# A 3x3 convolution with residual add: weights loaded on 128 partitions from another queue, the first image load split by columns over two queues, six early stores instead of five

## The chip, the cores and the metric

The kernel runs on one core of a Trainium2 chip. The metric is the device time of one execution in microseconds (us); medians are given with the lowest and highest of the runs. A profiled execution also gives the span, from its first to its last instruction. For the kernel before the time is about 2.1 us above the span.

## The reference

```python
def reference(x, weight, residual):      # x, residual [16, 64, 64, 64] f32; weight [64, 64, 3, 3] f32
    ... # pad x by one pixel on each side
    output[b, co] += weight[co, ci, kh, kw] * x_pad[b, ci, kh:kh+h, kw:kw+w]   # for all b, co, ci, kh, kw
    return (output + residual).astype(np.float32)
```

Each of x, residual and the output is 16.78 MB, the weights are 147 KB: 50.48 MB have to cross between HBM (the chip's main memory) and SBUF (the core's own memory, whose rows, 128 in the image tiles here, are called partitions).

## The kernel before

Images are worked on in pairs. A pair's image tile and residual tile are 128 partitions of 16 KB; the queue of SP, the sync engine, issues all loads and stores but that of the weights, which is on ScalarE's queue. ScalarE casts the image to bf16, TensorE multiplies, VectorE adds the product to the residual tile in place, and SP stores that tile. The parts that matter here:

```python
    ident = pool.tile([64, 64], FP32)
    ro = [pool.tile([128, NPIX], FP32, name=f"ro{p}") for p in range(NPAIR)]
    xr = [nc.alloc_sbuf_tensor(f"xr{i}", [128, NPIX], FP32) for i in range(NXR)]
    wraw = nc.alloc_sbuf_tensor("wraw", [64, 576], FP32)
    ...
        for p in range(NPAIR):                       # SP: all loads ...
            if p >= NXR:
                nc.sync.wait_ge(s_half, 2 * (p - NXR) + 3)
            i = load_x(p)
            if p == 0:
                to_the_front(i)                      # issued at entry, ahead of the start barrier
            load_ro(p)
        for p in range(NEARLY):                      # ... then five early stores
            nc.sync.wait_ge(s_add, 2 * p + 3)
            store(p).then_inc(s_out, 16)
    ...
        nc.scalar.dma_start(out=wraw[:, :], in_=w_flat[:, :]).then_inc(s_w, 16)
    ...                                              # VectorE: six weight casts out of PSUM
        for half, d, par, kh in blocks:
            i = nc.vector.tensor_copy(out=wl[hp, d, :, par, :], in_=tpf[0:64, 3 * kh : 3 * kh + 3, :])
    ...
    for p in range(NEARLY, NPAIR):                   # issued only when all compute is done
        store(p)
```

## Time and profile before

| | before |
|---|---|
| time, median (lowest to highest) | 124.1 us (124.02 to 124.42) |
| span | 122.1 us |
| bytes moved, steady rate | 50.48 MB, 429 GB/s |
| busy: PE, VectorE, ScalarE | 86.5, 75.2, 62.0 us |
| first packet starts, last data packet ends | 1.01 us, 120.75 us |

The page of the profile has one row of 40 slices for the DMA engines and one for their GB/s. The reading here is by stretches: wherever the rate is below 429 GB/s the stream loses time that it never gets back, because the transfers set the end. The trace also has a record for each packet, with its start, duration and size. A packet here is one row of a tile, mostly 16 KB. The lines are shown in the prediction.

### The profile page before, as it was taken

Reading aid. Unit: us, or ns where it says so; the run is one execution under the profiler, and the core shown is the slowest. Engines: PE = TensorE matmul, PEld = TensorE weight load, DVE = VectorE, ACT = ScalarE, POOL = GpSimd, SP = SyncE. Lnnn points to the kernel's source line nnn. Section 1 sums busy time; section 2 is a strip of 40 time slices with the busy share of each in tenths; the row PEclk is TensorE's granted clock in tenths of the full one; section 3 lists DMA queues with packets and bytes.
Section 4 is the critical chain, followed back from the end, with each engine's and each line's share of the span. In section 5 each row is a group of like instructions: output and inputs, shape, how many; then the busy total and the mean of one; then the engine's idle time right before and its main releaser. Section 6 shows DMA issues by size and latency. Waiting matters only on the chain.

```text
span 122.1 us, 729 instructions
## 1 busy us (share of the span) xinstructions
PE 86.5 (71%) x389; PEld 10.4 (9%) x105; DVE 75.2 (62%) x38; ACT 62.0 (51%) x33; POOL 2.2 (2%) x16
## 2 busy tenths in 40 slices
PE   0003799999999999999999999999999930000000
PEld 0003000101111010101010101111110100000000
DVE  0004101989889898898989889898798988000000
ACT  4009948966984993992994896699000000000000
POOL 5100000000000000000000000000000000000000
PEclk9999999999999999999999999999999999555555
DMA  6999999999999999999999999999999999999993
GB/s 182 408 348 429 429 429 429 429 424 429 429 429 424 429 429 429 429 429 429 429 429 419 429 429 424 429 429 429 435 435 435 429 429 429 435 435 429 429 429 140
DMA packets 3536, 50.48 MB, mean 413 GB/s; under 512 B 400, under 2 KB 400, under 8 KB 464
## 3 DMA queue, kind: packets, MB, share of 16 engines
q1 hardware_dynamic: 3456, 50.33, 97.8%
q10 hardware_dynamic: 80, 0.15, 0.4%
HBM read 33.70 MB, written 16.78 MB: 413 GB/s over the span
## 4 chain that ended last, share of the span: by engine, by line
PE 70%; DVEq 2%; DVE 2%; issue 0%
PE ps L84 53%; PE ps L83 17%; DVEq L118 2%; DVE ro L182 2%
## 5 line engine op out<-in xcount | busy, mean ns | idle before, releaser
L182 DVE TENSOR_TENSOR ro<-ps,ro 64x2048 f32<-64x2048 f32 x32 | 73.2, 2289 | 17.4 <-PE ps L84 16.9
L84 PE MATMUL ps<-xp,wl 128*128 128x504 bf16 (+1 forms) x288 | 79.9, 387 | 0.2
L159 ACT CAST xp<-xr 64x2048 bf16<-64x2048 f32 x16 | 30.3, 1896 | 21.3 <-DMA xr<-in_x_dram 21.1
L83 PE MATMUL ps<-xp,wl 128*128 128x504 bf16 (+1 forms) x92 | 35.6, 387 | 2.4 <-PEq L200 2.4
L163 ACT CAST xp<-xr 64x2048 bf16<-64x2048 f32 x16 | 30.4, 1897 | 0.4
L83 PEld LDWEIGHTS ps<-xp,wl 128*128 128x128 bf16 x96 | 9.5, 99 | 77.5 <-issue 77.5
L172 DVE CAST wl<-ps 64x192 bf16<-64x192 f32 x6 | 1.9, 347 | 10.9 <-PE ps L195 10.8
L195 PE MATMUL ps<-ident,wraw 64*64 64x64 f32 x9 | 1.1, 305 | 9.6 <-DMA wraw<-in_weight_dram 9.6
L159 ACT ACT_TABLE_LOAD x1 | 1.3, 1283 | 1.5 <-SPq L118 1.5
L195 PEld LDWEIGHTS ps<-ident,wraw 64*64 64x64 f32 x9 | 0.9, 163 | 9.6 <-issue 9.6
L146 POOL MEMSET xp<- 64x64 bf16 x4 | 0.6, 147 | 0.2
L145 POOL MEMSET xp<- 64x64 bf16 x4 | 0.6, 145 | 0.2
L148 POOL MEMSET wl<- 64x192 bf16 x1 | 0.3, 253 | 0.1
L147 POOL MEMSET wl<- 64x192 bf16 x1 | 0.3, 252 | 0.1
L135 POOL TENSOR_SCALAR_AFFINE_SELECT ident<-ident 64x64 f32<-64x64 f32 x1 | 0.2, 233 | 0.2 <-POOL ident L133 0.2
L133 POOL MEMSET ident<- 64x64 f32 x1 | 0.1, 145 | 0.5 <-SPq L118 0.5
L235 POOL MEMSET const-bfloat16-1.0<- 128x1 bf16 x1 | 0.1, 113 | 0.0
L235 POOL MEMSET const-uint8-127<- 128x1 uint8 x1 | 0.1, 112 | 0.0
L235 POOL MEMSET const-float32-1.0<- 128x1 f32 x1 | 0.1, 109 | 0.0
L235 POOL MEMSET const-float32-0.0<- 128x1 f32 x1 | 0.1, 104 | 0.2 <-issue 0.2
## 6 DMA issues: line engine op xcount, KB each, us to landing
xr<-in_x_dram SPq DMA_DIRECT2D x8, 2048.0 KB, 17.6
ro<-in_residual_dram SPq DMA_DIRECT2D x8, 2048.0 KB, 22.1
out_dram<-ro SPq DMA_DIRECT2D x8, 2048.0 KB, 28.7
wraw<-in_weight_dram ACTq DMA_DIRECT2D x1, 144.0 KB, 8.5
```

What stands on the lines that cost most here:

```text
L83: return e.matmul(out=out_, lhsT=lhsT, rhs=rhs, start=start, stop=stop, skip_group_check=True)
L84: return e.add_instruction(mybir.InstMatmult(name=nc.get_next_instruction_name(), engine=PE, ins=[e.lower_ap(rhs), e.lower_ap(lhsT)], outs ...
L118: with tc.tile_critical(no_gpsimd_drain=True):
L145: nc.gpsimd.memset(t[0:64, 0, :], 0.0).then_inc(s_id, 1)
L146: nc.gpsimd.memset(t[64:128, J, :], 0.0).then_inc(s_id, 1)
L147: nc.gpsimd.memset(wl[0:64, 0, :, 1, :], 0.0).then_inc(s_id, 1)
L159: i = nc.scalar.copy(out=t[64:128, 0:J, :], in_=x4[hp, :, 0, :])
L163: nc.scalar.copy(out=t[0:64, 1 : J + 1, :], in_=x4[hp, :, 1, :]).then_inc(s_pack, 1)
L172: i = nc.vector.tensor_copy(out=wl[hp, d, :, par, :], in_=tpf[0:64, 3 * kh : 3 * kh + 3, :])
L182: i = nc.vector.tensor_tensor(out=o4[hp, :, par, :], in0=psj[64 * par : 64 * par + 64, :, :], in1=o4[hp, :, par, :], op=ADD)
L195: i = nc.tensor.transpose(out=ps[0][0:64, t // 8, t % 8, :], in_=wraw3[:, :, t], identity=ident[:, :])
L235: nc = _bacc.Bacc("TRN2", target_bir_lowering=False, num_devices=1)
```

## The change

Its intent: load the weights through all 128 partitions and early on SP's queue, share the first image load between both queues, prepare the weights on VectorE and ScalarE together, and keep one more store in the queue at the end.

```diff
-    NEARLY = 5
+    NEARLY = 6
-    w_flat = weight.rearrange("co ci kh kw -> co (ci kh kw)")
+    w_rows = weight.rearrange("co (h ci) kh kw -> (co h) (ci kh kw)", h=2)
-    ident = pool.tile([64, 64], FP32)
+    ident = pool.tile([128, 128], FP32)
-    wraw = nc.alloc_sbuf_tensor("wraw", [64, 576], FP32)
+    wraw = nc.alloc_sbuf_tensor("wraw", [128, 288], FP32)
...
-            i = load_x(p)
             if p == 0:
-                to_the_front(i)
+                to_the_front(load_x(p, cols=slice(0, NPIX // 2)))
+                nc.sync.dma_start(out=wraw[:, :], in_=w_rows[:, :]).then_inc(s_w, 16)
+            else:
+                load_x(p)
...
+        nc.gpsimd.wait_ge(s_id, 2)
...
-        nc.scalar.dma_start(out=wraw[:, :], in_=w_flat[:, :]).then_inc(s_w, 16)
+        to_the_front(load_x(0, nc.scalar, slice(NPIX // 2, NPIX)))
...
+            if n == 0:                               # ScalarE: four of the twelve weight casts
+                nc.scalar.wait_ge(s_wt, 1)
+                for b in blocks[4:]:
+                    for h in range(2):
+                        i = nc.scalar.copy(**weight_block(h, *b))
+                i.then_inc(s_wt, 1)
...
+        for k, b in enumerate(blocks[:4]):           # VectorE: eight of them
+            for h in range(2):
+                i = nc.vector.tensor_copy(**weight_block(h, *b))
...                                                  # nine transposes of 128x32 instead of 64x64
+        nc.tensor.wait_ge(s_wt, 3)
```

More of the change, by code (lines that the diff above doesn't have):

```diff
@@ L68, with load_x @@
     s_add = sem("s_add")
-    def load_x(p):
-        return nc.sync.dma_start(out=xr[p % NXR][:, :], in_=x_bc[128 * p : 128 * p + 128, :]).then_inc(s_x[p % NXR], 16)
+    def load_x(p, engine=nc.sync, cols=slice(0, NPIX)):
+        return engine.dma_start(out=xr[p % NXR][:, cols], in_=x_bc[128 * p : 128 * p + 128, cols]).then_inc(
+            s_x[p % NXR], 16
+        )
     def load_ro(p):
@@ L113, in to_the_front, with weight_block @@
         at = next(
-            i for i, e in enumerate(front) if e.engine == mybir.EngineType.SP and isinstance(e, mybir.InstDrain)
+            i for i, e in enumerate(front) if e.engine == ins.engine and isinstance(e, mybir.InstDrain)
         )
         front.insert(at, copy.replace(ins, ins=[fixed(a) for a in ins.ins], outs=[fixed(a) for a in ins.outs]))
+    blocks = ((0, 0, 0, 0), (1, 0, 0, 1), (1, 0, 1, 0), (0, 1, 1, 1), (0, 1, 0, 2), (1, 1, 1, 2))
+    tp = ps[0].rearrange("p c j w -> p c (j w)")
+    def weight_block(h, half, d, par, kh):
+        at = 64 * half + 32 * h
+        return dict(out=wl[at : at + 32, d, :, par, :], in_=tp[0:32, kh, 0:384].rearrange("p (kw co h) -> p kw co h", kw=3, h=2)[:, :, :, h])
     with tc.tile_critical(no_gpsimd_drain=True):
@@ L140 @@
             base=0,
-            pattern=[[-1, 64]],
+            pattern=[[-1, 128]],
             channel_multiplier=1,
         ).then_inc(s_id, 1)
+        nc.gpsimd.wait_ge(s_id, 2)
         for t in xp:
@@ L157 @@
             if im == 0:
-                nc.scalar.wait_ge(s_x[p % NXR], 16 * (p // NXR + 1))
+                nc.scalar.wait_ge(s_x[p % NXR], 16 * (p // NXR + 1 + (p % NXR == 0)))
             i = nc.scalar.copy(out=t[64:128, 0:J, :], in_=x4[hp, :, 0, :])
@@ L163 @@
             nc.scalar.copy(out=t[0:64, 1 : J + 1, :], in_=x4[hp, :, 1, :]).then_inc(s_pack, 1)
-        nc.vector.wait_ge(s_wt, 1)
-        tpf = ps[0].rearrange("p c j w -> p (c j) w")
-        blocks = ((0, 0, 0, 0), (1, 0, 0, 1), (1, 0, 1, 0), (0, 1, 0, 2), (0, 1, 1, 1), (1, 1, 1, 2))
-        for half, d, par, kh in blocks:
-            hp = slice(64 * half, 64 * half + 64)
-            i = nc.vector.tensor_copy(out=wl[hp, d, :, par, :], in_=tpf[0:64, 3 * kh : 3 * kh + 3, :])
-        i.then_inc(s_bank, 2)
+            if n == 0:
[4 more added lines that the diff above has]
+                i.then_inc(s_wt, 1)
+        nc.vector.wait_ge(s_wt, 1)
+        for k, b in enumerate(blocks[:4]):
+            for h in range(2):
+                i = nc.vector.tensor_copy(**weight_block(h, *b))
+                if k == h == 0:
+                    i.then_inc(s_bank, 2)
+        i.then_inc(s_wt, 1)
         for n in range(B):
@@ L194 @@
         for t in range(9):
-            i = nc.tensor.transpose(out=ps[0][0:64, t // 8, t % 8, :], in_=wraw3[:, :, t], identity=ident[:, :])
+            i = nc.tensor.transpose(
+                out=tp[0:32, t // 3, 128 * (t % 3) : 128 * (t % 3) + 128], in_=wraw3[:, :, t], identity=ident[:, :]
+            )
         i.then_inc(s_wt, 1)
+        nc.tensor.wait_ge(s_wt, 3)
         with nc.Fori(0, B // NXP, 1, engines=[PE]):
```

## The prediction

The sum: -0.43 us for the weights, +0.10 for the packets and -0.10 for the split, together -0.43, from 124.1 to 123.7 us. The weights' term stands as the estimate, 80% of the 0.54 us that the trace loses between 5.8 and 8.9 us. The low end of the range, 123.1, was for all of that gain and a faster start.

> **What bounds the kernel now.** I read the summary page first: its row of slices, its queues and its groups.
>
> ```profile
> span 122.1 us, 729 instructions
> ...
> DMA  6999999999999999999999999999999999999993
> GB/s 182 408 348 429 429 429 429 429 424 429 429 429 424 429 429 429 429 429 429 429 429 419 429 429 424 429 429 429 435 435 435 429 429 429 435 435 429 429 429 140
> ...
> q1 hardware_dynamic: 3456, 50.33, 97.8%
> q10 hardware_dynamic: 80, 0.15, 0.4%
> ...
> L182 DVE TENSOR_TENSOR ro<-ps,ro 64x2048 f32<-64x2048 f32 x32 | 73.2, 2289 | 17.4 <-PE ps L84 16.9
> ```
>
> The transfers are the bound. All 40 slices but the first and last have the DMA engines at 90% or more, and from the fourth slice on they move 429 GB/s without a break. The program moves 50.48 MB whatever the compute does; at 429 GB/s that is 117.7 us of the 122.1 us span. PE, VectorE and ScalarE are busy for 86.5, 75.2 and 62.0 us, all of it beside the transfers. So only three things can move the end: when the first byte starts, how many bytes' worth of time the stream loses on its way, and what follows the last byte.
>
> The second view is the table of stretches of time (columns: stretch, its length, busy us of PE, PE loads, VectorE, ScalarE, GpSimd with instruction counts, granted clock, DMA share, GB/s).
>
> ```profile
> 1.00:3.00 2.00, 0.00 (x0) 0.00 (x0) 0.00 (x0) 1.28 (x1) 1.39 (x10) 1.00 1.03 270
> 3.00:5.80 2.80, 0.00 (x0) 0.00 (x0) 0.00 (x0) 0.00 (x0) 0.60 (x3) 1.00 0.97 409
> 5.80:8.90 3.10, 0.00 (x0) 0.00 (x0) 0.00 (x0) 0.01 (x1) 0.00 (x0) 1.00 1.03 354
> 8.90:12.00 3.10, 1.14 (x9) 0.93 (x9) 1.16 (x4) 3.08 (x2) 0.00 (x0) 1.00 0.99 423
> 12.00:119.80 107.80, 85.40 (x380) 9.52 (x96) 74.01 (x35) 57.61 (x31) 0.00 (x0) 0.92 1.01 429
> ```
>
> The stream loses time in two places, both before 9 us. **Start:** the first packet begins at 1.06 us; from then to 3.00 at 429 GB/s would be 832 KB, 540 KB were moved, so 0.68 us are lost, and from 3.0 to 5.8 another 2.8 x 20/429 = 0.13. The transfer records (one for each packet, with start, duration and size) say why: the first packet on each engine takes 0.78 to 1.78 us, where a 16 KB packet later takes 0.611. **Weights:** from 5.8 to 8.9 the rate is 354, a loss of 3.1 x 75/429 = 0.54 us, although the share of busy engines is full. The weight packets (64 of 2304 B, on ScalarE's queue) begin at 5.25 and end at 8.31; in that time the 16 KB packets of the other queue stretch from 0.61 to 0.75-0.92 us, and they are back at 0.61 by 8.9. The loss goes with the weights, not with the image.
>
> The third view is the timeline, at the entry, the weight path, and the last issue of stores.
>
> ```profile
> 0.00 0.38 SPq L71 DMA_DIRECT2D xr<-in_x_dram  x1
> ...
> 0.95 0.53 ACTq L151 DMA_DIRECT2D wraw<-in_weight_dram  x1
> ...
> 8.89 1.90 ACT L159 CAST xp<-xr 64x2048 bf16<-64x2048 f32 x1 [6.09 <-DMA xr<-in_x_dram]
> 9.60 0.93 PEld L195 LDWEIGHTS ps<-ident,wraw 64*64 64x64 f32 x9 [9.60 <-issue]
> 9.63 1.14 PE L195 MATMUL ps<-ident,wraw 64*64 64x64 f32 x9 [9.63 <-DMA wraw<-in_weight_dram]
> 10.81 1.97 DVE L172 CAST wl<-ps 64x192 bf16<-64x192 f32 x6 [10.81 <-PE ps L195]
> ...
> 98.78 4.61 DVE L182 TENSOR_TENSOR ro<-ps,ro 64x2048 f32<-64x2048 f32 x2 [0.58 <-PE ps L84]
> 103.68 1.76 SPq L77 DMA_DIRECT2D out_dram<-ro  x3
> ```
>
> The compute chain (weights, transposes, casts, then matmuls without a gap from 13.1 to 98.8, last add done at 103.4) releases only the last three stores, issued at 103.68. The last packet of data ends at about 120.8; three stores are 6.29 MB or 14.7 us, so the queue still holds earlier stores until about 106.1. With 1.06 us from issue to first packet, as at the entry, the compute chain has some 1.4 us of slack before the queue runs dry. From the last data to the end of the span is 1.3 us; the timed 124.1 is 2.0 above the span.
>
> [...] In this trace the issue takes 0.38 us and is followed by 0.7 us before the first packet, so the split of the first load has little to save.
>
> **The change part by part.**
> *Weights on 128 partitions.* The same 147 KB as 128 packets of 1152 B. [...]most of its 0.54 us goes; I count 80% of it, -0.43. More packets cost their fixed part: a 2304 B packet undisturbed takes 93 ns, against 86 ns at the rate of 16384 B in 611; so some 8 ns a packet. Four more weight packets on each engine, eight more from the halved image rows and one more semaphore write are 13 x 8 ns = +0.10. The weights are issued second by SP, at about 1 us, and the residual load about 0.5 us later than now; the queue holds 2 MB of image (4.9 us) by then, so this is hidden.
> *Image 0 by columns on both queues, at entry.* 128 packets of 8 KB on each queue instead of 128 of 16 KB. Bytes and engines are the same. Each engine could have the slow first packets of two queues open together. If the first-packet delay is a latency, it overlaps and nothing is won or lost; if it grows with size, up to 0.3 is won. I count -0.10.
> *Weight preparation.* Nine transposes stream 128 columns instead of 64: the present pitch is (1.14 - 0.3)/8 = 0.11 us, doubled 0.21, so about 1.14 + 9 x 0.105 = 2.1 us, +0.95. The casts become 12 of 32x192; [...]0.347 us each by the group of L172 (1.97 us for six in a row, 0.33 apart). VectorE does eight: 2.6 us, +0.7. ScalarE does four after its two image casts: about 4 x 0.35 = 1.4 us (an estimate from VectorE's). PE now waits for both. With the image landing about 1.2 us earlier (7.7: no weights among it) and weights about 8: transposes to 10.1, VectorE to 12.7; ScalarE 7.7 + 3.8 = 11.5, then to 12.9. So matmuls begin near 13.0 instead of 13.1, or up to 1 us later if the loads don't come earlier. Either way it is off the path that sets the end, as long as the final stores are issued in time.
> *Six early stores.* Store 5 needs thirteen semaphore counts, which VectorE gives at 103.4 - 3 x 5.19 - 2.3 = 85.5 us. It is then in the queue long before its turn, and only two stores wait for the end of the program's compute block: two are 9.8 us, so the slack grows from 1.4 to about 6.3 us. It gains nothing now; it keeps the queue full if the stream moves forward by 0.5 us or the compute chain back by 1 us.
> *Sum:* -0.43 + 0.10 - 0.10 = -0.43 us, from 124.1 to **123.7 us**. The whole that could be had here is the 0.68 + 0.13 + 0.54 = 1.35 us lost at the head, which is 1.1%.
>
> **The rivals.**
> *Small packets or two queues[...] cost the time.* The slow stretch may come from an engine alternating between two queues, or from small packets as such. For: the stretch is the only time in the trace when two queues run together. Against: the first dozen weight packets, 5.25 to 5.6 us, leave the 16 KB packets at 0.611. Then the change makes it worse: 16 packets an engine alternate in the image instead of four, or twice as many small packets run; losing the 0.54 again once over gives 124.6.
> *The start is what improves.* Two queues bring twice the first packets; if the 0.7 us is per packet and not per engine, the stream fills about 0.3 to 0.5 us sooner[...]. Against: the first 16 packets already occupy all 16 engines at 1.06 to 1.5 us.
> *The compute chain becomes the bound.* If matmuls began 1 us later with five early stores, the queue would run dry for a few tenths; with six there are over 5 us to spare, so this rival gives +0.
> *Nothing shows.* The runs before spread from 124.02 to 124.42, as wide as my gain.
>
> **Range and chances.** [...]the loss of the first rival in part 124.4; I put 8 in 10 on 123.1 to 124.4. Two per cent is 2.5 us: below 121.6 would need more than all head losses together, above 126.6 a stall that I see no cause for. Chances: faster 0.02, same 0.96, slower 0.02.
>
> **What would show it.** In the changed profile the third slice should be near 420 GB/s instead of 348, and the stretch from 5.8 to 8.9 us above 410, with 16 KB packets at 0.61 us; the first ScalarE cast should start near 7.7 instead of 8.89; transposes should take about 2.1 us; the first conv matmul should begin at 12.9 to 14; the late slices should stay at 429 with two stores issued near 104; and the last data should end about 0.4 us earlier. I am wrong if the rate still sags while the weights are moved, if the first slices are slower with two queues, if first packets appear much later or earlier than 1.06 us, or if the rate drops after 104 us.

## The result

The kernel after takes **122.98 us** (122.92 to 123.00, six runs), against 124.10 before (124.02 to 124.42, six runs). The ratio is 0.9905, 95% interval 0.9892 to 0.9918. Ratios are computed as the mean time of one kernel's runs over that of the other's of the same rounds, so they are not quite the ratio of the medians quoted. The prediction said 123.7 in a range of 123.1 to 124.4: the direction was right, the gain was more than twice the forecast, and the time fell just outside the range.

The page of the kernel after, in the rows that answer to those of before:

```profile
span 121.2 us, 736 instructions
...
DMA  6999999999999999999999999999999999999993
GB/s 168 427 444 433 433 433 433 433 427 433 433 427 427 433 433 427 427 433 427 433 433 433 433 433 422 433 389 433 433 433 433 422 433 433 433 433 433 427 433 151
...
q1 hardware_dynamic: 3600, 49.43, 96.3%
q10 hardware_dynamic: 144, 1.05, 2.0%
...
L189 DVE CAST wl<-ps 32x192 bf16<-32x192 f32 x8 | 2.8, 348 | 10.4 <-PE ps L214 10.3
...
L182 ACT CAST wl<-ps 32x192 bf16<-32x192 f32 x4 | 1.2, 306 | 0.0
```

The third slice rose from 348 to 444 GB/s. The first slice fell from 182 to 168, and the first row below from 270 to 254, though the prediction named slower first slices as a sign of being wrong. It isn't one: these views count a packet's bytes where it starts, so the long packets of before count earlier. By the packets' ends 0.5 MB had passed at 3.29 us, against 3.58 before. There is a new dent (the word for this loss below), 389 GB/s in the 27th slice (about 79 to 82 us), that before doesn't have. (The 433 against 429 in the other slices is no rate: slices are shorter with a shorter span, and the same packets fall into each.) The queue of ScalarE, q10, now carries half an image pair.

The table of stretches of the kernel after (columns as in the prediction: the last one is GB/s):

```profile
1.00:3.00 2.00, 0.00 (x0) 0.00 (x0) 0.00 (x0) 1.28 (x1) 1.32 (x8) 1.00 0.95 254
3.00:5.80 2.80, 0.00 (x0) 0.00 (x0) 0.00 (x0) 0.00 (x0) 0.85 (x5) 1.00 1.00 421
5.80:8.90 3.10, 0.76 (x4) 0.58 (x5) 0.00 (x0) 1.13 (x1) 0.00 (x0) 1.00 1.06 439
8.90:12.00 3.10, 1.32 (x7) 0.58 (x4) 1.60 (x5) 3.06 (x4) 0.00 (x0) 1.00 1.01 433
```

The stretch from 5.8 to 8.9 us, where the weights pass, went from 354 to 439 GB/s: the sag is gone.

The timeline of the kernel after (columns: start, us, engine, line, operation, what ended the idle time before):

```profile
0.00 0.38 SPq L71 DMA_DIRECT2D xr<-in_x_dram  x1
0.13 0.36 ACTq L71 DMA_DIRECT2D xr<-in_x_dram  x1
...
7.77 1.90 ACT L173 CAST xp<-xr 64x2048 bf16<-64x2048 f32 x1 [5.41 <-DMA xr<-in_x_dram]
...
8.14 2.08 PE L214 MATMUL ps<-ident,wraw 128*32 128x128 f32 x9 [8.14 <-DMA wraw<-in_weight_dram]
...
10.33 2.90 DVE L189 CAST wl<-ps 32x192 bf16<-32x192 f32 x8 [10.33 <-PE ps L214]
11.50 1.26 ACT L182 CAST wl<-ps 32x192 bf16<-32x192 f32 x4
...
13.66 0.59 PE L85 MATMUL ps<-xp,wl 128*128 128x512 bf16 x1 [3.44 <-PEq L222]
...
104.42 0.96 SPq L79 DMA_DIRECT2D out_dram<-ro  x2
```

The image lands 1.1 us earlier and the weights 1.5 us earlier, but their preparation takes longer, so the matmuls begin 0.5 us *later* than before and the last stores are issued 0.7 us later. None of this empties the queue: by the packet records some packet is always moving between the first and the last.

**Where the time came from.** From the packet records one can say when the first N MB had been moved:

| moved | before | after | difference |
|---|---|---|---|
| 1.5 MB | 5.96 us | 5.67 us | -0.29 |
| 4 MB (weights past) | 12.38 | 11.56 | -0.82 |
| 32 MB (end of loads) | 77.74 | 76.57 | -1.17 |
| 33.8 MB (first stores) | 81.92 | 81.08 | -0.84 |
| last data packet | 120.75 | 119.87 | -0.89 |

So 0.29 us is won at the start, 0.53 at the weights and 0.35 little by little over the long load phase (in before the packets are slightly longer there, which is called the creep below), and 0.33 is given back where loads turn into stores. The span is 0.9 us shorter (122.1 to 121.2). The time is 1.12 us shorter; the rest is outside the span: 124.16 us with a span of 122.1 in the profiled execution before, 123.00 with 121.2 after, so 2.1 and 1.8 us.

A second sum shows the same from the packets: what the 16 KB packets took over 611 ns, added up and divided by 16 engines. I call it the **stretch**, and it is used for every experiment below. The halved rows of the first load, 8 KB, are not in it; after 4 us they take a median of 309 ns in the kernel after, about half of 611.

| kernel | 4 to 12 us | 12 to 74 us | 74 to 84 us |
|---|---|---|---|
| before | 0.57 | 0.37 | 0.05 |
| after (its profile in a second job) | 0.00 (0.00) | 0.00 (0.00) | 0.36 (0.16) |
| w64_sp_only | 0.73 | 0.38 | 0.06 |
| w128_act_only (second job) | 0.00 (0.00) | 0.00 (0.00) | 0.09 (0.34) |
| after_nosplit | 0.01 | 0.00 | 0.13 |
| split_only | 0.44 | 0.39 | 0.05 |
| split_both_sp | 0.00 | 0.00 | 0.49 |
| before_shift128 | 0.49 | 0.06 | 0.01 |
| before_shift256 | 0.61 | 0.37 | 0.05 |
| after_shift128 | 0.00 | 0.28 | 0.06 |
| after_all256 | 0.00 | 0.00 | 0.30 |

### The profile page after: what moved, and what is told of

Same layout as the page of the kernel before. It is cut to its first block, busy times and chain, and to the rows that moved or that the text cites. A ratio compares the mean times of both kernels' runs of the same rounds, so it can differ in the third digit from the quotient of the medians. Undisturbed runs are those within 1.5% of the kernel's fastest.

```text
span 121.2 us, 736 instructions
## 1 busy us (share of the span) xinstructions
PE 87.7 (72%) x389; PEld 10.7 (9%) x105; DVE 76.0 (63%) x40; ACT 63.1 (52%) x37; POOL 2.4 (2%) x16
## 4 chain that ended last, share of the span: by engine, by line
PE 71%; DVEq 2%; DVE 2%; issue 0%
PE ps L86 53%; PE ps L85 17%; DVEq L129 2%; DVE ro L201 2%
## 5 line engine op out<-in xcount | busy, mean ns | idle before, releaser
L189 DVE CAST wl<-ps 32x192 bf16<-32x192 f32 x8 | 2.8, 348 | 10.4 <-PE ps L214 10.3
L214 PE MATMUL ps<-ident,wraw 128*32 128x128 f32 x9 | 2.1, 412 | 8.1 <-DMA wraw<-in_weight_dram 8.1
L214 PEld LDWEIGHTS ps<-ident,wraw 128*32 128x32 f32 x9 | 1.2, 137 | 8.6 <-issue 8.1
L182 ACT CAST wl<-ps 32x192 bf16<-32x192 f32 x4 | 1.2, 306 | 0.0
```

What stands on the lines that cost most here:

```text
L182: i = nc.scalar.copy(**weight_block(h, *b))
L189: i = nc.vector.tensor_copy(**weight_block(h, *b))
L214: i = nc.tensor.transpose(out=tp[0:32, t // 3, 128 * (t % 3) : 128 * (t % 3) + 128], in_=wraw3[:, :, t], identity=ident[:, :])
```

## The experiments

Theory at the outset: the 64-partition weight load was what slowed the stream at 5.8 to 8.9 us. Rivals: two alternating queues, or small packets as such. Open besides: what the split does, whether the sixth store matters, and the creep. There were eighteen runs, all with correct results; times are medians, and each is compared with runs of before on the same chip.

| run | time (lowest to highest) | ratio to before, 95% interval |
|---|---|---|
| w128_act_only | 122.78 (122.72 to 122.85) | 0.9890 [0.9876, 0.9905] |
| w64_sp_only | 124.28 (124.10 to 124.72) | 1.0014 [0.9998, 1.0030] |
| after_nosplit | 123.09 (122.78 to 123.15) | 0.9904 [0.9890, 0.9917] |
| split_only | 126.15 (125.41 to 126.75) | 1.0163 [1.0133, 1.0194] |
| before_early6 | 124.42 (123.97 to 124.49) | 1.0025 [1.0012, 1.0037] |
| after_early5 | 123.19 (122.84 to 123.55) | 0.9924 [0.9907, 0.9941] |
| split_both_sp | 123.14 (122.88 to 123.44) | 0.9926 [0.9911, 0.9940] |
| split4_sp | 123.53 (123.31 to 123.63) | 0.9952 [0.9940, 0.9964] |
| mid128 | 124.11 (123.74 to 124.49) | 0.9981 [0.9962, 1.0001] |
| mid64 | 124.35 (124.23 to 124.84) | 1.0023 [1.0002, 1.0044] |
| w128_act_again | 123.13 (122.91 to 123.29) | 0.9907 [0.9886, 0.9928] |
| after_again | 122.92 (122.90 to 123.06) | 0.9899 [0.9879, 0.9920] |
| before_shift128 | 123.77 (123.60 to 124.26) | 0.9970 [0.9951, 0.9989] |
| after_shift128 | 122.97 (122.90 to 123.00) | 0.9900 [0.9882, 0.9918] |
| before_shift256 | 124.12 (124.07 to 124.23) | 0.9995 [0.9980, 1.0011] |
| after_all256 | 123.04 (122.86 to 123.32) | 0.9903 [0.9885, 0.9921] |

(Two more, before_ident128 and after_all_dve, are at the end.)

### Partitions or queue: w64_sp_only and w128_act_only

Together with before and after_nosplit these fill a square: weights on 64 or 128 partitions, on ScalarE's or on SP's queue.

```diff
# w64_sp_only, against before
+                nc.sync.dma_start(out=wraw[:, :], in_=w_flat[:, :]).then_inc(s_w, 16)   # second on SP
-        nc.scalar.dma_start(out=wraw[:, :], in_=w_flat[:, :]).then_inc(s_w, 16)
# w128_act_only, against after: the first image load whole on SP, and
-                nc.sync.dma_start(out=wraw[:, :], in_=w_rows[:, :]).then_inc(s_w, 16)
+        nc.scalar.dma_start(out=wraw[:, :], in_=w_rows[:, :]).then_inc(s_w, 16)
```

> The kernel before with only the weights' queue changed: still 64 partitions of a whole row, but issued second on SP's queue. Theory[...]: the sag stays (about 350 GB/s for some 3 us), time within 0.2 us of before. Rival 'two queues': the sag is gone, 0.5 us faster.

> The kernel after without the split of the first image load, and with the weights (128 partitions of half a row) back on ScalarE's queue. Theory[...] (64 partitions were the cost): the sag between 5.8 and 8.9 us is gone (over 410 GB/s instead of 354) though two queues still alternate; 0.4 to 0.6 us faster than before. Rival 'two queues or small packets': the sag stays or deepens, time 124.1 or more.

The stretch of 5.8 to 8.9 us in w64_sp_only:

```profile
5.80:8.90 3.10, 0.00 (x0) 0.00 (x0) 0.00 (x0) 0.49 (x1) 0.00 (x0) 1.00 1.03 312
```

and in w128_act_only:

```profile
5.80:8.90 3.10, 0.00 (x0) 0.00 (x0) 0.00 (x0) 0.93 (x1) 0.00 (x0) 1.00 1.02 429
```

With 64 partitions on one single queue the sag is deeper (312 against 354 GB/s); with 128 partitions on the second queue, and twice as many packets of half the size, there is none. The time follows: no gain for the first, all of the gain for the second. The rivals of queues and of small packets fall; of what was tried the number of partitions is what counts (a stretch of 0.57 and 0.73 us with 64, of 0.01 and 0.00 with 128).

### The same cost in the middle of the stream: mid128 and mid64

```diff
# against after; (p, c) is (128, 576) or (64, 1152), 295 KB that nobody uses
+            if p == 3:
+                nc.sync.dma_start(out=spare[:, :], in_=res_bc[0:p, 0:c]).then_inc(s_d, 16)
```

> The kernel after plus one load that nobody uses: 295 KB of the residual into a spare tile on 128 partitions of 2304 B, in the middle of the stream (on SP's queue behind the fourth residual tile). Both theories: the bytes alone cost 0.69 us at 429 GB/s, so 0.7 to 0.8 us slower than after; 16 KB packets stay at 611 ns afterwards.

> The same 295 KB, but on 64 partitions of 4608 B: half as many, longer packets. Theory[...]:[...] 1.4 us or more slower than after, packets stretch around 30 to 40 us. If a 64-partition load also leaves the engines in the slower rhythm, 16 KB load packets go from 611 to 614.7 ns from then on (another 0.2 us) and the time outside the span rises from 1.8 to 2.1 us. Rival 'small packets were the cost': 0.7 us or less, faster than mid128.

By 20 MB, that is after the extra load and with its bytes counted as moved, mid128 is 0.43 us behind after and mid64 0.95 (0.32 and 0.84 behind the profile of after from the same job). So the 64-partition form costs 0.52 us more at the spot, although its packets are twice as long: the packets of the spare tile took 1.02 us of 16 engines against 0.85, and those around them stretch by 0.50 against 0.08. Both expectations were off in size: mid128 lost more than its bytes (its time is 1.19 us above after's in the same job, not 0.7), and mid64 only 0.24 more than that (1.43 above after). The 1.4 us expected for mid64 was the author's assumption; no run before it had shown such a cost. In the profile of mid128, as far as the packets' times tell the sixteen DMA engines apart (the records name none), fourteen end by 120.42 us and two at 120.80 and 121.36, where all sixteen of after end between 119.30 and 119.87: here the ends are uneven after the extra load, and the last packet sets the end. So 64 partitions cost more than 128 in both places, 0.57 us of stretch against 0.00 at the weights and 0.50 against 0.08 here. Why they do is not visible in a trace.

### The split: after_nosplit, split_only, split_both_sp, split4_sp

```diff
# after_nosplit, against after
-                to_the_front(load_x(p, cols=slice(0, NPIX // 2)))
+                to_the_front(load_x(p))
-        to_the_front(load_x(0, nc.scalar, slice(NPIX // 2, NPIX)))
# split_only, against before
+                to_the_front(load_x(p, cols=slice(0, NPIX // 2)))
+        to_the_front(load_x(0, nc.scalar, slice(NPIX // 2, NPIX)))     # ahead of the weights
# split_both_sp, against after: both halves from SP; split4_sp: four quarters from SP
```

> The kernel after with the first image load whole on SP's queue. The time until byte N of the two traces says the split gave about 0.3 us in the first 1.5 MB: so 0.3 us slower than after, about 0.8 us faster than before, first packets again of 0.8 to 1.8 us. If the split does nothing (the prediction counted 0.1): within 0.1 us of after.

> The kernel before with only the first image load split over both queues; weights stay on 64 partitions on ScalarE's queue. If the split's gain adds to the weights' gain: 0.3 us faster than before (123.8), with the sag near 350 GB/s still there. If the split does nothing: 124.1.

> The kernel after with both column halves of the first image load issued by SP at entry instead of one by ScalarE. In the trace after, ScalarE's queue sends its first packet only at 2.67 us, when the slow first packets are over. Theory 'the smaller first packets give the 0.3 us at the start, not the second queue': by 1.5 MB still 0.25 to 0.35 us ahead of before, time within 0.15 of after. Rival 'the second queue gives it': 0.3 us behind after at 1.5 MB.

> As split_both_sp, but the first image load is cut into four column quarters (4 KB packets), all on SP at entry. If smaller first packets are what helps, the start gains another 0.1 to 0.2 us by 0.5 MB, against 24 more packets per engine at 8 ns (0.2 us) for the whole load: by 2 MB level with split_both_sp, time 122.8 to 123.1. If not, 0.2 us slower than after.

At 1.5 MB the kernels stand, against before, at -0.04 us (after_nosplit), -0.39 (split_only), -0.36 (split_both_sp), -0.29 (after). So the split does win 0.3 us at the start, and it is the shorter rows that win it: the second queue isn't needed, and in the kernel after its first packet starts only at 2.67 us. The first 16 packets take 0.78 to 1.78 us in before, and 0.31 to 1.30 in after with rows of half the length. Quarters win nothing: split4_sp, whose first 16 packets take only 0.16 to 0.59 us, is level with before at 1 MB and 0.21 us behind at 1.5 MB. SP needs 1.81 us to issue the four loads; that this is the reason is not shown.

In the *time* this start is not seen. The kernels after and after_nosplit, from two jobs, have ratios of 0.9905 and 0.9904, each uncertain by 0.0013 (0.16 us). In the profiles the difference goes where loads turn into stores: packets stretch by 0.13 us without the split and by 0.36 with it, and by 0.49 in split_both_sp. In the second job after had 0.16 there and w128_act_again 0.34, so this loss varies from run to run, and I don't know what sets it.

The largest effect of the round is that of split_only, 2 us slower. The timeline of split_only, at the weights and the last stores:

```profile
13.10 1.14 PE L199 MATMUL ps<-ident,wraw 64*64 64x64 f32 x9 [13.10 <-DMA wraw<-in_weight_dram]
...
16.59 0.58 PE L85 MATMUL ps<-xp,wl 128*128 128x512 bf16 x1 [2.35 <-PEq L204]
...
106.61 1.77 SPq L79 DMA_DIRECT2D out_dram<-ro  x3
```

Its table of stretches, where before has 459 and 410 GB/s:

```profile
105.00:106.00 1.00, 0.00 (x0) 0.00 (x0) 1.00 (x1) 0.00 (x0) 0.00 (x0) 0.93 0.16 66
106.00:107.00 1.00, 0.00 (x0) 0.00 (x0) 0.32 (x1) 0.00 (x0) 0.00 (x0) 0.50 0.00 0
```

The weights wait behind half an image on ScalarE's queue, and TensorE has them at 13.10 instead of 9.63 us. Matmuls begin 3.5 us later and the three last stores are issued at 106.61 instead of 103.68. The five early stores are used up at 105.73, the first packet of the next starts at 107.44, and between them the queue stands empty for 1.7 us. I had expected 123.8: this is the rival "the compute chain becomes the bound", and it is real. The kernel after escapes it twice: its weights are second on SP's queue, and it has a sixth early store. w128_act_only shows the second escape alone: its last stores are issued at 106.56 us, as late as in split_only, but with six early stores its queue never runs dry (at least 425 GB/s in every microsecond from 104 to 112).

### The sixth store: before_early6 and after_early5

```diff
-    NEARLY = 5        # before_early6; after_early5 has it the other way round
+    NEARLY = 6
```

> The kernel before with six early stores instead of five, nothing else. In both kernels with five early stores the timed figure is 2.0 to 2.1 us above the span, in the kernels with six 1.8. Theory 'the sixth early store takes 0.2 us off outside the span': span as before (122.1), time 0.2 us less (123.9). Rival 'that 0.2 us comes with the weights' 128 partitions': time equal to before.

> The kernel after with five early stores. The compute chain issues its last stores at about 104.4 us and the first packet comes 1 us later; five early stores end at about 105.3 in the trace after. Theory 'the sixth store covers the later compute chain': the queue runs dry for 0.1 to 0.4 us, time 123.2 to 123.6. Rival 'the sixth store does nothing': 123.0.

Alone the sixth store gains nothing: before_early6 is 0.3 us slower by ratio, which I can't explain, with the same 2.1 us outside the span. In the kernel after, going back to five gives 0.9924 against 0.9905. These 0.2 us are not clear of noise: the intervals overlap, and split_both_sp, in the same job and with six early stores, has 0.9926. What five stores do is seen in the profile of after_early5, the slowest of its six runs. Its table of stretches:

```profile
104.00:105.00 1.00, 0.00 (x0) 0.00 (x0) 0.41 (x1) 0.00 (x0) 0.00 (x0) 0.97 0.28 115
```

From 105.04 to 105.55 us no packet moves at all; in the kernel after the same microsecond has 459 GB/s. So the sixth store is cover, not gain, as predicted; what the cover is worth in this kernel's median time is not shown.

### The creep: before_shift128, after_shift128, before_shift256, after_all256

Up to here every kernel with 64-partition weights had about 614.7 ns as the mean of a 16 KB packet between 12 and 74 us, every one with 128 had 611.0. But mid64, with a 64-partition load in its middle, went back to 611 to 612 behind it. Something else came with the weight tiles: the weight tile shrank from 2304 to 1152 bytes a partition and the identity grew from 256 to 512. The residual tiles behind them moved by 1152 + 512 - 2304 - 256 = -896 bytes, or 3.5 times 256: in the built programs they start at 68224 before (128 past a multiple of 256) and at 67328 after (a multiple of 256). The image tiles start at 16512, 128 past, in both.

```diff
# before_shift128: an unused tile behind wraw; before_shift256 has 64 columns, after_shift128 has 32
+    pad = nc.alloc_sbuf_tensor("pad", [128, 32], FP32)
# after_all256: the same, and one ahead of the image tiles
+    pad0 = nc.alloc_sbuf_tensor("pad0", [128, 32], FP32)
```

> The kernel before with an unused tile of 128 bytes a partition behind the weight tile; residual tiles then start at a multiple of 256 as in after. Theory 'layout': 16 KB load packets go from 614.7 to 611.0 ns between 12 and 74 us, span and time fall by some 0.35 us (with the time outside the span, if it is layout too, 0.6 us): 123.5 to 123.8. The sag between 5.8 and 8.9 us stays[...]; if it goes too, it was layout. Rival 'the 64-partition transfer sets the rhythm': 124.1, 614.7 ns.

> The kernel after with an unused tile of 128 bytes, so that residual tiles start 128 bytes past a multiple of 256 as in before. Theory 'layout': packets go to 614.7 ns, 0.3 to 0.6 us slower than after (123.3 to 123.6). Rival: 123.0, 611.0 ns.

> Control: the kernel before with an unused tile of 256 bytes, which keeps the residual tiles 128 bytes past a multiple of 256. Both theories: 124.1, 614.7 ns. If this is faster too, it isn't the alignment but some other shift.

> The kernel after with the three image tiles moved to a multiple of 256 too (in before and after they start 128 bytes past one). If their alignment matters beside the residual's, a further gain, at most some 0.3 us (122.7); their packets already take 611.0 ns in after, so I expect no more than 0.1 us from it.

The table of stretches of before_shift128 (the row from 12 to 76 us, which before has at 428 GB/s, and the row of the weights):

```profile
5.80:8.90 3.10, 0.00 (x0) 0.00 (x0) 0.00 (x0) 0.01 (x1) 0.00 (x0) 1.00 1.04 366
...
12.00:76.00 64.00, 62.99 (x283) 7.14 (x72) 50.59 (x24) 50.05 (x27) 0.00 (x0) 1.00 1.01 430
```

The layout is the cause of the creep, as the shift alone takes it away; of the tiles that it moves only the residual tiles are filled and emptied by DMA. The shift of 128 takes its stretch from 0.37 to 0.06 us and the time down by 0.3% (0.9970, interval clear of 1); the control shift of 256 does nothing. The opposite shift brings the creep into the kernel after (0.28). The sag at the weights stays in before_shift128 (366 GB/s, stretch 0.49), so layout is not its cause.

But after_shift128 isn't slower than after: 122.97 us. It loses 0.28 in the load phase and then passes the turn from loads to stores with 0.06 instead of 0.36. In the row from 76 to 84 us, the kernel after:

```profile
76.00:84.00 8.00, 8.00 (x39) 0.88 (x9) 6.81 (x4) 7.59 (x4) 0.00 (x0) 1.00 0.98 399
```

So of what the change won, the creep nets about nothing, and the theory's 0.3 to 0.6 us for after_shift128 failed. Aligning the image tiles too gave nothing (123.04).

### Outside the span: before_ident128 and after_all_dve

In all kernels above the time is 2.03 to 2.14 us above the span with the old weight part, and 1.74 to 1.86 with the new one, in every single run. Two runs looked for the piece that carries it.

```diff
# before_ident128, against before
+    ident = pool.tile([128, 128], FP32)      # and GpSimd's added wait
# after_all_dve, against after: ScalarE's four weight casts go to VectorE
-                for b in blocks[4:]:
-                    for h in range(2):
-                        i = nc.scalar.copy(**weight_block(h, *b))
+        for k, b in enumerate(blocks):
```

> The kernel before with the identity at 128x128 and GpSimd's added wait (layout keeps its alignment: 128 bytes past a multiple of 256). If GpSimd's part carries the 0.25 us: timed figure 1.8 us above the span, time 123.9. If not: 2.1 above, 124.1.

> The kernel after with all twelve weight casts on VectorE, none on ScalarE. If ScalarE's casts carry the 0.25 us: timed figure 2.1 above the span, time 123.2. If not: 1.8, 123.0. The matmuls begin about 1.4 us later (twelve casts of 0.35 instead of eight), which the six early stores should cover at no cost.

before_ident128: 124.21 us, still 2.02 to 2.13 above the span (ratio 1.0001). So GpSimd's part doesn't carry it. after_all_dve: 123.50 us (123.29 to 123.78), ratio 0.9955; its spans are 121.1 to 121.6, near those of after, but its time is 2.18 to 2.21 us above them. Its matmuls begin at 15.19 us, 1.5 later than in after, and that costs nothing in the profiled span, as expected.

By the figure set beforehand this speaks for ScalarE's casts. The trace speaks against it. It also records the changes of semaphores (the counters by which engines wait for each other) after the last instruction, in a closing sequence that every profile has. In the 19 others this sequence ends 1.91 to 1.95 us after the span, in before (1.94) as in after (1.95). In after_all_dve it ends 2.34 us after it, with a gap of 0.50 us between two changes that are 0.10 apart in all the others. Later in the same sequence, at 122.74 to 123.12 us, comes one packet of 8 KB that no other profile has at its end, on a queue that the kernel doesn't issue on (the view of after_all_dve's DMA queues between 119 and 125 us shows it):

```profile
q14 instruction: 1, 0.01, 0.4%
```

So after_all_dve has a delay of its own, 0.40 us; without it its profiled run would be some 1.82 us above the span (2.22 - 0.40), like after (1.83) and not like before (2.06). The run met its forecast for another reason, and ScalarE's casts are probably not what the 0.25 us are. What makes the delay is not shown. Which piece of the weight part carries the 0.25 us stays open too: it isn't in the closing sequence, which is as long in before as in after, and the sixth store isn't it (after_early5 is 1.81 to 1.86 above its spans).

### One chip for two candidates: w128_act_again and after_again

> The kernel of w128_act_only again, to compare it with after on one chip. If the split gives nothing in the end: 0.1 to 0.3 us below after (122.7 to 122.9), as in the first round. If the first round's difference was the chip's: equal.

> The kernel after itself, for the same comparison: 122.9 to 123.1 us.

In the first round w128_act_only, without the split, had the lowest time of all. Beside after on one chip it doesn't hold: 123.13 against 122.92, with intervals that overlap. No version tried beats the kernel after clear of the spread.

## Why the prediction was right or wrong

- **What bounds the kernel: right.** The transfers set the end in every run but split_only and the profiled one of after_early5, where their queue ran dry. Where the compute chain came later by 0.5 to 3.7 us it cost nothing while stores were queued, and it cost 2 us in split_only where they were not.
- **Weights on 128 partitions: right that the 64 partitions cost (why is not shown), undersized.** I counted 80% of a 0.54 us sag and took off 0.10 for the fixed part of more packets, -0.33 net. Measured: between 1.5 and 4 MB after gains 0.53 us net, and the stretch there goes from 0.57 to 0.00. All of the sag went, and the packet cost didn't show.
- **The split: undersized at the start, and then not seen in the time.** I counted -0.10, with up to 0.3 if the first-packet delay grows with size. From 16 to 8 KB it does (first 16 packets 0.78 to 1.78 us against 0.31 to 1.30): -0.29 at 1.5 MB, and split_both_sp shows that size and not the second queue does it. after_nosplit has the same ratio as after, so at the end of the run this gain isn't visible.
- **Weight preparation: right.** Predicted transposes 2.1 us, VectorE casts 2.6, ScalarE casts 1.4, image at 7.7, weights at about 8, matmuls at 12.9 to 14. Measured 2.08, 2.8 (2.90 from first to last), 1.2 (1.26), 7.77, 8.14 and 13.66. The cast of 32x192 on VectorE takes 348 ns, where 64x192 took 347: here half the partitions at the same 192 elements took the same time.
- **Six early stores: right** that it gains nothing and covers the rest; the slack was small enough for the profile of after_early5 to show it.
- **The step that failed** is the sum, "-0.43 + 0.10 - 0.10 = -0.43 us, from 124.1". Its terms for the weights and the start were 0.20 and 0.19 us too small. And it carried "the timed 124.1 is 2.0 above the span" over unchanged: that difference fell by 0.25 us in every run with the new weight part. I took it for a constant because only one kernel had been seen; what moves it stays open (before_ident128 excludes GpSimd's part, and the trace of after_all_dve speaks against ScalarE's casts). Also missing were the creep (-0.35) and the dent at the turn to stores (+0.33), which cancel. From the profiles: -0.29 - 0.53 - 0.35 + 0.33 - 0.05 (from the first stores to the last packet) = -0.89, and -0.25 outside the span make -1.14, against -1.12 by the medians.
- **"The whole that could be had here is ... 1.35 us ... at the head"** was wrong as a bound: it left out the long load phase, where 428 GB/s was not the ceiling (432 in after, from 12 to 76 us), and the time outside the span. It took the 429 GB/s of the steady slices for the most that can be had there, and 0.611 us for the 16 KB packet of the whole run, where its mean in before between 12 and 74 us is 0.6147.
- **Small misreadings.** The prediction's packet times (1.06, 5.25, 8.31, 120.8) are 0.05 us late against the span's start (1.01, 5.20, 8.26, 120.75). "The first 16 packets already occupy all 16 engines" holds for fifteen, which start by 1.43 us; the next starts at 1.96. Neither changes the sum.
- **Rivals.** "Small packets or two queues" fell with w64_sp_only and w128_act_only. "The start is what improves" was half right: the start won 0.29 us, but by shorter rows, not by a second queue. "Nothing shows" was wrong: the interval of the ratio, 0.9892 to 0.9918, is clear of 1. "The compute chain becomes the bound" was right as a danger and averted in this change.

## What to carry to other kernels

When transfers are the bound, look for stretches in which packets take longer than their steady duration, and ask which transfer was beside them: here a load of 147 KB on 64 partitions, worth 0.34 us at 429 GB/s, stretched its neighbours by another 0.57. Reordering loads moves the compute chain too, so keep enough stores queued to cover it before touching the order. A tile whose size changes moves the tiles behind it (here by 896 bytes); run a control that only shifts memory before crediting a steady change in rate to anything else.
